# A shared selector for both halves of the state-space mask, and expert 0's rows from one-hot products

## The chip, the core and the metric

The kernel runs on one core of one Trainium2 chip. A core has five engines, each with an instruction queue of its own: TensorE (PE, matmuls and transposes; PEld is its loading of the stationary operand), VectorE (DVE), ScalarE (ACT), GpSimd (POOL) and SyncE (SP, which here only issues DMAs). They wait for each other through semaphores. The metric is the device time of one execution in microseconds; lower is better.

## The reference

The program is two transformer blocks on 512 tokens of width 1024. Only what the change touches is shown, shortened:

```python
# block 1, state-space part (SSD): 12 heads in 4 groups of 3, 4 chunks of 128 tokens
a_cs = cumsum(da)                                          # per chunk and head
seg  = a_cs[..., :, None] - a_cs[..., None, :]
lmat = exp(where(causal, seg, -inf))                       # 128 x 128 per chunk and head
y_diag = einsum('bclgn,bcsgn->bcgls', cm, bm) * lmat ...   # "mask" times C.B, then times x

# block 2, mixture of experts: 16 experts, 2 per token
h = h + concat(o_a, o_b) @ w_out
t = rms_norm(h, ffn_norm)
gates = route(t @ w_group + b_group, t @ w_expert + b_expert)
for e in range(16):
    y += gates[:, e:e+1] * ((silu(t @ w_gate[e]) * (t @ w_up[e])) @ w_down[e])
return rms_norm(h + y, final_norm)
```

## The kernel before

Large products work on weights in units of 512 KB (128 x 1024 fp32). SP loads a unit into a ring of `raw` buffers; ACT copies it to a reduced-precision half `whi` and DVE (or POOL) subtracts to get the rest, `wlo` (`split`, L264). Each product is then three matmuls, hi x hi, hi x lo, lo x hi (`mm3`, L274, lines 276 to 278). The loads run ahead of the splits, and the splits ahead of PE, as far as the rings have room (`fill`). The recorded instructions are put in order by a scheduler that knows costs and priorities; `issue_after` makes an instruction stand behind another, and `ahead(n)` raises its priority.

**The mask units** (`ssd_dt`, `ssd_mask_unit`, L776 to L848). `ssd_dt` transposes the 48 running sums (4 chunks x 12 heads) of a token chunk into rows, splits them into hi and lo parts, and spreads each over three columns of heads: `ssd_cH` and `ssd_cL`, 48 x 384 each. A selector `ssd_sel` (48 x 16, ones in the three rows that belong to a unit) picks a unit's rows. For each of 16 units PE sums into one bank: the causal mask (L840), selector x hi (L841), selector x lo (L842), and beside it C.B (L843). ACT then takes the exponent and DVE multiplies.

**From w_out_2 to expert 0** (L2005 to L2175). w_out_2 is computed in two halves of 512 columns (`projR`, L378). As each of four token tiles of the second half is added to `x` on DVE (L403), `after(tt)` transposes it, computes routing logits (`logits`: 4 fp32 matmuls of 20 columns against `rt_w`, L2028), the norm factor (`rstd`, with a power on POOL, L291) and the tile's choice of experts (`route_tile`). `ranks(tt)` counts the place of each token among its expert's tokens and makes the one-hot matrix `rt_oh` of expert 0: token by slot, 96 slots (L2049, bf16). Each tile of x times the norm gain is written to a DRAM table `xnd`.

After the fourth tile, `slots_row(0)` multiplies the one-hot with token numbers (L1833) to get the 96 row numbers `sn_i`, POOL gathers these rows from `xnd` into `ex_g` by an indirect DMA, PE transposes them (8 transposes, L1887), and ACT and DVE split them into `ex_xh` and `ex_xl`, on which expert 0's gate products run. The same is done for expert 1 (`sn_oh`, L2098). A small DMA `mark` writes expert 0's row numbers to DRAM (L2116) so that the weight loads behind it on SP wait until the numbers exist. Two weight splits have their `wlo` on POOL in this stretch (`s.plan`, L2088). `final_norm` is loaded as one row (`grow`) and spread over partitions by two fp32 matmuls against ones (L125). Later experts' rows are gathered two experts ahead, from the indices `sn_ix` that `route` computes.

Of the kernel before, what the change touches and what calls it, by code (L numbers as in the profile page):

```python
# [70 lines left out]
class Kern:  # L71
# [202 lines left out]
    def mm3(s, ps, a, asl, b, bsl, first, last):  # L274
        mm = s.nc.tensor.matmul
        mm(ps, a.hi[asl], b.hi[bsl], start=first, stop=False)  # L276
        mm(ps, a.hi[asl], b.lo[bsl], start=False, stop=False)  # L277
        mm(ps, a.lo[asl], b.hi[bsl], start=False, stop=last)  # L278
# [99 lines left out]
    def projR(s, src, ld, nk, get, x, after, tail=3, mid=None, lag=2, order=None):  # L378
# [4 lines left out]
        for half in range(2):  # L383
            cs = slice(half * 512, half * 512 + 512)
# [16 lines left out]
            for tt in range(NT):  # L401
                mms(ws, tt)
                nc.vector.tensor_add(x[:, tt, cs], x[:, tt, cs], pss[tt])  # L403
# [372 lines left out]
    def ssd_dt(s, pd, x):  # L776
# [32 lines left out]
        it = s.tmp.tile([48, 16], F32, name="ssd_it", tag="h")  # L809
        nc.gpsimd.iota(it, pattern=[[-3, 16]], base=0, channel_multiplier=1, allow_small_or_imprecise_dtypes=True)  # L810
        eq = s.tmp.tile([48, 4, 16], F32, name="ssd_eq", tag="h")
# [15 lines left out]
        for o, v in ((s.ssd_cs.hi, hi), (s.ssd_cs.lo, lo)):
            V.tensor_mul(o, v.bitcast(F32)[:, None, :].to_broadcast(sh), hm[:, :, None].to_broadcast(sh))
        yield

    def ssd_mask_unit(s, pl, c, g):
# [7 lines left out]
        sel = s.ssd_sel[:, u:u + 1].to_broadcast([48, P])  # L839
# [895 lines left out]
    def route(s, pool, tmp, g, ev):  # L1735
# [58 lines left out]
        for i in range(2):  # L1794
# [3 lines left out]
        V.tensor_tensor(oh, s.slot[:, None, :].to_broadcast([P, 8, CAP]),  # L1798
                        rk.rearrange("p i t -> p (i t)")[:, :, None].to_broadcast([P, 8, CAP]), OP.is_equal)
# [28 lines left out]
    def slots_row(s, pool, e, oh):  # L1828
# [7 lines left out]
        if e:  # L1836
            nc.scalar.activation(v, ps[:CAP, 0:2], AF.Copy)
        else:
            nc.vector.tensor_copy(v, ps[:CAP, 0:2])
        eng = nc.gpsimd if e else nc.vector  # L1840
        s.row_op = eng.tensor_scalar(ix, v[:, 0:1], v[:, 1:2], float(T), op0=OP.add, op1=OP.add).ins
# [138 lines left out]
    def moe(s, mixT):  # L1980
# [35 lines left out]
        oh = pr.tile([P, NT, CAP], BF16, name="rt_oh")  # L2016
# [76 lines left out]
        ix = []
        for e in range(XG):
            if e:
                oh = pn.tile([P, NT, CAP], BF16, name="sn_oh")
                sh = [P, NT, CAP]
                V.tensor_tensor(oh, s.slot[:, None, :].to_broadcast(sh), s.rk[:, :, e:e + 1].to_broadcast(sh), OP.is_equal)  # L2098
# [3 lines left out]
            if not e:  # L2102
                s.fence = [s.row_op]
        grow = s.tmp.tile([1, D], F32, name="grow", tag="h", bufs=1)
        with s.tc.issue_after(hi_op):
            nc.scalar.dma_start(grow, dap(A["final_norm_2"], 0, [[D, 1], [1, D]]))
        with s.tc.issue_after(s.logit_op), s.tc.issue_after(hi_op):
            gf = s.bcast_pe(s.gain, grow, "gain")
# [6 lines left out]
        mark = s.dram.tile([CAP, 1], I32, name="mark")  # L2115
# [212 lines left out]
```

## Time and profile before

| | |
|---|---|
| Median of 3 runs | 1455.51 us (1454.84 to 1457.64) |
| Profiled execution | 1453.98 us, its span 1452.2 us |
| PE busy | 1399.7 us, 96% of the span |
| DVE, ACT, POOL busy | 977.7, 779.2, 103.8 us |
| Chain that ended last, by engine | PE 86%, DVE 6%, ACT 3%, DMA 2% |
| Mean granted clock of PE | 0.987 |

A span is the time from the first to the last instruction of one execution that the profiler recorded. A busy share is an average over the whole program; what a stretch is bound by is read from that stretch. The chain starts at the last instruction and follows back what each step waited for. "issue to landing" of a DMA is the time from its issue until its completion is seen. The granted clock is PE's clock as a share of full speed; its two levels are 1.2 and 2.4 GHz.

### The profile page before, as it was taken

The numbers are of one execution on the slowest core, as the hardware profiler recorded it, in microseconds if no ns is written. First come the engines' busy times: TensorE is split into PE (matmuls) and PEld (weight loads), VectorE is DVE, ScalarE is ACT, GpSimd is POOL, SyncE is SP. The second block draws the span as 40 slices with busy tenths as digits, with TensorE's granted clock in tenths as the row PEclk, the third lists the DMA queues.
The fourth block names the chain that finished last, engine by engine and source line by source line (L and its number), as shares of the span: only waits on it lengthen the run. The fifth ranks groups of instructions, "written<-read, shape, count | busy, mean of one in ns | idle before, by whom it ended". The sixth has DMA issues, their size and how long they took to land.

```text
span 1452.2 us, 20178 instructions
## 1 busy us (share of the span) xinstructions
PE 1399.7 (96%) x7467; PEld 1130.2 (78%) x7467; DVE 977.7 (67%) x1772; ACT 779.2 (54%) x1200; POOL 103.8 (7%) x103
## 2 busy tenths in 40 slices
PE   7999999999999999999999999999998599999996
PEld 6888887787879888888888889877887367777774
DVE  6989577565465444444365997766555599999997
ACT  6465654434334333233344685554443388888885
POOL 1000000010010000000000400000102111111111
PEclk9999999999999999999999999999999699999998
DMA  7353342521223333323232423120754899999993
GB/s 199 92 136 112 90 131 73 174 88 58 75 71 116 102 95 94 101 88 100 89 101 87 134 74 88 41 77 18 260 204 172 226 357 356 353 343 349 349 349 130
DMA packets 145933, 223.51 MB, mean 154 GB/s; under 512 B 18466, under 2 KB 71106, under 8 KB 145816
## 3 DMA queue, kind: packets, MB, share of 16 engines
q1 hardware_dynamic: 136852, 200.48, 42.7%
q0 software_dynamic: 3568, 10.34, 3.0%
q10 hardware_dynamic: 5412, 11.37, 2.2%
q8 instruction: 59, 0.97, 0.3%
q14 instruction: 42, 0.34, 0.1%
HBM read 208.41 MB, written 14.95 MB: 154 GB/s over the span
## 4 chain that ended last, share of the span: by engine, by line
PE 86%; DVE 6%; ACT 3%; DMA 2%; issue 2%; POOL 1%; DVEq 0%; SPq 0%; ACTq 0%; POOLq 0%
PE mm L276 24%; PE mm L278 24%; PE mm L277 24%; PE sm L1416 2%; PE tr L1548 1%; PE tr L323 1%; PE tr L1887 1%; PE sm L1532 1%; POOL rs_r L291 1%; DMA ex_g<-xnd,sn_i 1%; DVE wlo L271 1%; PE sm L879 1%; PE sm L276 1%; PE tr L1540 1%; PE sm L2028 1%
## 5 line engine op out<-in xcount | busy, mean ns | idle before, releaser
L271 DVE TENSOR_TENSOR wlo<-raw,whi 128x1024 fp32r<-128x1024 f32 (+1 forms) x351 | 423.6, 1222 | 216.4 <-ACT whi L270 213.5
L270 ACT ACTIVATE whi<-raw 128x1024 fp32r<-128x1024 f32 (+1 forms) x356 | 372.7, 1057 | 293.2 <-PE mm L277 154.0
L276 PE MATMUL mm<-hT_hi,whi 128*128 128x512 f32 (+1 forms) x768 | 283.2, 369 | 1.9 <-DVE x L403 1.7
L278 PE MATMUL mm<-hT_hi,wlo 128*128 128x512 f32 (+1 forms) x768 | 281.5, 367 | 0.0
L277 PE MATMUL mm<-hT_lo,whi 128*128 128x512 f32 (+1 forms) x768 | 280.9, 366 | 0.0
L276 PE MATMUL mm<-whi,hT_hi 128*128 128x512 f32 (+1 forms) x592 | 219.7, 371 | 1.4 <-ACT hT_hi L315 1.4
L278 PE MATMUL mm<-whi,hT_lo 128*128 128x512 f32 (+1 forms) x592 | 217.9, 368 | 0.0
L277 PE MATMUL mm<-wlo,hT_hi 128*128 128x512 f32 (+1 forms) x592 | 217.0, 367 | 0.0
L278 PEld LDWEIGHTS mm<-hT_hi,wlo 128*128 128x128 f32 x768 | 144.7, 188 | 24.3
L276 PEld LDWEIGHTS mm<-hT_hi,whi 128*128 128x128 f32 x768 | 144.3, 188 | 24.8 <-DVE x L403 1.9
L277 PEld LDWEIGHTS mm<-hT_lo,whi 128*128 128x128 f32 x768 | 144.6, 188 | 23.3
L276 PEld LDWEIGHTS mm<-whi,hT_hi 128*128 128x128 f32 x592 | 111.8, 189 | 20.7 <-ACT hT_hi L315 2.3
L278 PEld LDWEIGHTS mm<-whi,hT_lo 128*128 128x128 f32 x592 | 111.7, 189 | 19.2 <-issue 0.6
L277 PEld LDWEIGHTS mm<-wlo,hT_hi 128*128 128x128 f32 x592 | 112.0, 189 | 18.5 <-issue 1.0
L276 PE MATMUL mm<-whi,ex_xh 128*96 128x512 f32 x256 | 102.8, 402 | 1.3 <-ACT ex_xh L315 0.6
L291 POOL TENSOR_TENSOR rs_r<-rs_v,mhalf 128x1 f32<-128x1 f32 (+2 forms) x42 | 33.4, 798 | 980.2 <-DVE rs_v L289 823.9
L277 PE MATMUL mm<-wlo,ex_xh 128*96 128x512 f32 x256 | 101.4, 396 | 0.0
L278 PE MATMUL mm<-whi,ex_xl 128*96 128x512 f32 x256 | 100.9, 395 | 0.0
L276 PEld LDWEIGHTS mm<-whi,ex_xh 128*96 128x96 f32 x256 | 41.5, 162 | 19.0 <-ACT ex_xh L315 1.1
L278 PEld LDWEIGHTS mm<-whi,ex_xl 128*96 128x96 f32 x256 | 41.6, 162 | 18.1
L277 PEld LDWEIGHTS mm<-wlo,ex_xh 128*96 128x96 f32 x256 | 41.8, 163 | 16.9
L1246 DVE SCALAR_TENSOR_TENSOR cv<-mm,cols,cv 128x511 f32<-128x511 f32 (+1 forms) x44 | 33.0, 749 | 30.0 <-ACT cv L1243 29.2
(568 smaller groups left out, 2060.3 us busy)
## 6 DMA issues: line engine op xcount, KB each, us to landing
raw<-in_w_gate SPq DMA_DIRECT2D x64, 512.0 KB
raw<-in_w_up SPq DMA_DIRECT2D x64, 512.0 KB
raw<-in_w_down SPq DMA_DIRECT2D x64, 512.0 KB
raw<-in_ffn_w_up SPq DMA_DIRECT2D x44, 512.0 KB
raw<-in_w_in SPq DMA_DIRECT2D x40, 512.0 KB
raw<-in_ffn_w_down SPq DMA_DIRECT2D x22, 512.0 KB
raw<-in_w_out SPq DMA_DIRECT2D x16, 512.0 KB
raw<-in_w_in SPq DMA_DIRECT2D x8, 520.0 KB
```

The costliest lines, as they stand in the source:

```text
L270: s.hi_op = s.nc.scalar.activation(hv, v, AF.Copy).ins
L271: eng.tensor_sub(lv, v, hv.bitcast(F32))
L276: mm(ps, a.hi[asl], b.hi[bsl], start=first, stop=False)
L277: mm(ps, a.hi[asl], b.lo[bsl], start=False, stop=False)
L278: mm(ps, a.lo[asl], b.hi[bsl], start=False, stop=last)
L291: s.pow_op = nc.gpsimd.tensor_tensor(r, v, s.mhalf[:, :n], OP.pow).ins
L323: nc.tensor.transpose(ps[:, i * P:(i + 1) * P], src[:, (k0 + i) * P:(k0 + i + 1) * P], s.ident)
L879: nc.tensor.matmul(yd[:, o:o + 64], L[:, j], xdt[:, h], start=True, stop=True)
L1246: V.scalar_tensor_tensor(y[:, d:], ps[:, :512 - d], cw[:, w:w + 1], y[:, d:], op0=OP.mult, op1=OP.add)
L1416: nc.tensor.matmul(ps[:, sl], qk[:, sl], qk[:, sl], start=True, stop=True)
L1532: nc.tensor.matmul(ps[:, :n], qa[:, h, sl], ka[:, h, :n], start=True, stop=False)
L1540: nc.tensor.transpose(pt[:, j * P:j * P + P], p[:, j * P:j * P + P], s.ident)
```

## The change

The state-space part keeps hi and lo rows in one tile: the 48 sums are copied twice into a zeroed 128 x 128 tile (columns 0 to 47 and 64 to 111), transposed at once, and the upper 64 rows take the hi part, the lower 64 the lo part. The selector has 128 rows with the same ones in both halves, so one matmul of 128 rows takes the place of the two of 48.

Expert 0's rows are no longer gathered. The one-hot matrix of expert 0 is kept in fp32 and multiplied with x itself: `first(tt)` has 8 fp32 matmuls per tile (stationary: 128 columns of x, moving: the tile's 96 one-hot columns) that accumulate over the four tiles into two banks `p0` the transposed rows of expert 0. ACT and DVE take them out in 8 pieces each, with the norm gain as a scale, into `ex_xh` and `ex_xl`. Expert 1 is gathered as before; its one-hot is made tile by tile beside that of expert 0, and its row numbers are made on DVE. `mark`, the first gather, its transposes and the wide one-hot are gone; the two `wlo` that POOL made are made on DVE, behind the additions of tiles 0 and 1; `final_norm` is spread by one DMA on POOL's queue behind the last power. The one-hot of the 8 remaining parts of `route` now stands behind expert 1's row numbers, and expert 1's transposes behind a product of expert 0.

```diff
-        pt = s.ptr.tile([P, 512], F32, name="tr")
-        nc.tensor.transpose(pt[:48, 0:P], cs[:, 0].rearrange("p a b -> p (a b)"), s.ident)
...
+        c2 = s.tmp.tile([P, P], F32, name="ssd_c2", tag="h")
+        V.memset(c2, 0.0)
+        for r in (0, 64):
+            V.tensor_copy(c2[:, r:r + 48], cs[:, 0].rearrange("p a b -> p (a b)"))
         pt = s.ptr.tile([P, 512], F32, name="tr")
+        nc.tensor.transpose(pt[:, 0:P], c2, s.ident)
...
-        nc.tensor.matmul(o, sel, s.ssd_cs.hi.rearrange("p j t -> p (j t)"), start=False, stop=False)
-        nc.tensor.matmul(o, sel, s.ssd_cs.lo.rearrange("p j t -> p (j t)"), start=False, stop=True)
+        nc.tensor.matmul(o, s.ssd_sel[:, u:u + 1].to_broadcast([P, P]), s.ssd_cs.rearrange("p j t -> p (j t)"),
+                         start=False, stop=True)
...
+        def first(tt):
+
+            for b in range(2):
+                for k in range(4):
+                    c = (4 * b + k) * P
+                    nc.tensor.matmul(p0[b][:, k * CAP:(k + 1) * CAP], x[:, tt, c:c + P], oh[0][:, tt],
+                                     start=tt == 0 and k == 0, stop=tt == 3 and k == 3)
...
-            V.tensor_scalar(oh[:, tt], s.slot, s.rk[:, tt, 0:1], None, op0=OP.is_equal)
+            for e in range(2):
+                V.tensor_scalar(oh[e][:, tt], s.slot, s.rk[:, tt, e:e + 1], None, op0=OP.is_equal)
...
+            if tt == 3:
+                p0.extend(s.pmm.tile([P, 512], F32, name="mm") for _ in range(2))
+                for i in range(3):
+                    first(i)
...
+        gf = s.gain.tile([P, D], F32, name="gain")
+        with s.tc.issue_after(s.pow_op):
+            nc.gpsimd.dma_start(gf, dap(A["final_norm_2"], 0, [[0, P], [1, D]]))
         ranks(3)
+        first(3)
...
-        s.plan = [(nc.gpsimd, []), (nc.gpsimd, [s.pow_op])]
+        s.plan = [(V, [s.add_ops[0]]), (V, [s.add_ops[1]])]
+        late, s.late = s.late, 1000
         s.fill(most=L3, splits=2)
...
-            with s.tc.issue_after(s.rank_op):
-                ix.append(s.slots_row(pn, e, oh))
-            s.gather(xgs[e], ix[e])
...
+        with s.tc.issue_after(s.rank_op):
+            ix1 = s.slots_row(pn, 1, oh[1])
+        s.gather(xgs[1], ix1)
...
-        mark = s.dram.tile([CAP, 1], I32, name="mark")
-        with s.tc.issue_after(nc.sync.dma_start(mark, ix[0]).ins):
-            s.fill()
+        s.fence = [s.row_op]
+        s.fill()
         s.late = FL[5]
-        xT = s.expert_pick(pe, xgs[0])
+        xT = s.expert_xT(pe)
+        for k in range(KD):
+            ps = p0[k // 4][:, k % 4 * CAP:k % 4 * CAP + CAP]
+            gk = s.cols2[:, 96 + k:97 + k]
+            nc.scalar.activation(xT.hi[:, k], ps, AF.Copy, scale=gk)
+            V.scalar_tensor_tensor(xT.lo[:, k], ps, gk, xT.hi[:, k].bitcast(F32), op0=OP.mult, op1=OP.subtract)
...
-            xT = s.expert_pick(pe, xgs[(e + 1) % XG])
+            with s.tc.issue_after(s.gate_op) if e == 0 else nullcontext():
+                xT = s.expert_pick(pe, xgs[(e + 1) % XG])
```

The order of the instructions moves with this. The first place is a mask unit on PE; `neg_lt` is the causal mask, `BT` and `CT` are the B and C of the chunk. Before:

```order
755 L864 MATMUL tr<-ident,BT 128x128 x4
756 L840 LDWEIGHTS identb
757 L840 MATMUL sm<-neg_lt,identb 128x384
758 L841 MATMUL sm<-ssd_cH,ssd_sel 128x384
759 L842 MATMUL sm<-ssd_cL,ssd_sel 128x384
760 L843 MATMUL sm<-CT,BT 128x128
761 L276 MATMUL mm<-memT_hi,whi 128x256
```

And after the change:

```order
754 L872 MATMUL tr<-ident,BT 128x128 x4
755 L848 LDWEIGHTS identb
756 L848 MATMUL sm<-neg_lt,identb 128x384
757 L849 MATMUL sm<-ssd_cH,ssd_sel 128x384
758 L851 MATMUL sm<-CT,BT 128x128
759 L276 MATMUL mm<-memT_hi,whi 128x256
```

The unit has one matmul less, and nothing stands in its place.

The second place is PE from the last product of w_out_2 to expert 0's first gate products. `tr<-ident,x` are the transposes of tile 3, `rt_h` its transposed half for the logits, `rt_u` and `rt_o` belong to the ranks, `rt_tb` holds token numbers. Before:

```order
4916 L278 MATMUL mm<-whi,hT_lo 128x512
4917 L2023 MATMUL tr<-ident,x 128x128 x4
4918 L2028 MATMUL sm<-rt_w,rt_h 128x20 x4
...
4932 L1732 MATMUL sm<-rt_Mb,rt_u 128x16
...
4934 L1833 MATMUL sm<-rt_tb,rt_oh 96x2
...
4942 L1833 MATMUL sm<-rt_tb,sn_oh 96x2
...
4957 L125 MATMUL mm<-grow,ones 128x512 x2
4958 L1887 MATMUL tr<-ident,ex_g_9992 128x96 x8
4959 L276 MATMUL mm<-whi,ex_xh 96x512
4960 L277 MATMUL mm<-wlo,ex_xh 96x512
```

And after the change, where `rt_oh_9468` is the fp32 one-hot of expert 0 and `rt_oh_9469` the bf16 one of expert 1:

```order
4900 L278 MATMUL mm<-whi,hT_lo 128x512
4901 L2034 MATMUL mm<-rt_oh_9468,x 128x96 x15
4902 L2042 MATMUL tr<-ident,x 128x128 x4
4903 L2034 MATMUL mm<-rt_oh_9468,x 128x96
4904 L2047 MATMUL sm<-rt_w,rt_h 128x20 x4
...
4911 L2034 MATMUL mm<-rt_oh_9468,x 128x96 x8
...
4919 L1740 MATMUL sm<-rt_Mb,rt_u 128x16
...
4934 L2034 MATMUL mm<-rt_oh_9468,x 128x96 x8
...
4936 L1842 MATMUL sm<-rt_tb,rt_oh_9469 96x2
4937 L276 MATMUL mm<-whi,ex_xh 96x512
4938 L277 MATMUL mm<-wlo,ex_xh 96x512
4939 L278 MATMUL mm<-whi,ex_xl 96x512
```

Fifteen of the sixteen products of tiles 0 and 1 stand ahead of tile 3's transposes, tile 2's behind its ranks, tile 3's directly ahead of the gate; the matmuls on `grow` and the transposes of `ex_g` are gone.

The third place is DVE between the tables of tile 2 (`h`) and the addition of tile 3 (L403 before, L404 after). Before:

```order
1195 L2073 TENSOR_TENSOR h<-x,gain 128x1024
1196 L301 SCALAR_TENSOR_TENSOR rs_t<-rs_r,rs_h 128x1
1197 L306 SCALAR_TENSOR_TENSOR rt_r<-rs_t,rs_r 128x1
1198 L1733 TENSOR_TENSOR rt_rk<-sm,rt_Mb 128x16
1199 L2061 SCALAR_TENSOR_TENSOR rt_la<-sm,rt_r,rt_b 128x20
1200 L2049 TENSOR_SCALAR rt_oh<-rt_s,rt_rk 128x96
1201 L2063 SCALAR_TENSOR_TENSOR rt_lgg<-sm,rt_r,rt_la 128x4
1202 L2064 SCALAR_TENSOR_TENSOR rt_lge<-sm,rt_r,rt_la 128x16
1203 L1715 TENSOR_REDUCE rt_gm<-rt_lgg 128x1
1204 L403 TENSOR_TENSOR x<-x,mm 128x512
```

And after the change:

```order
1194 L2097 TENSOR_TENSOR h<-x,gain 128x1024
1195 L271 TENSOR_TENSOR wlo<-raw,whi 128x1024 x2
1196 L298 TENSOR_SCALAR rs_h<-rs_v 128x1
1197 L1741 TENSOR_TENSOR rt_rk<-sm,rt_Mb 128x16
1198 L301 SCALAR_TENSOR_TENSOR rs_t<-rs_r,rs_h 128x1
1199 L2069 TENSOR_SCALAR rt_oh_9468<-rt_s,rt_rk 128x96
1200 L306 SCALAR_TENSOR_TENSOR rt_r<-rs_t,rs_r 128x1
1201 L2069 TENSOR_SCALAR rt_oh_9469<-rt_s,rt_rk 128x96
1202 L2085 SCALAR_TENSOR_TENSOR rt_la<-sm,rt_r,rt_b 128x20
1203 L404 TENSOR_TENSOR x<-x,mm 128x512
```

The two `wlo` that POOL made stand here on DVE, ahead of tile 1's ranks and the addition of tile 3; the one-hot comparison stands there twice.

## Rows read from the trace of the kernel before

**Rows 1.** The page, busy shares by engine and the costliest group of instructions
```profile
PE 1399.7 (96%) x7467; PEld 1130.2 (78%) x7467; DVE 977.7 (67%) x1772; ACT 779.2 (54%) x1200; POOL 103.8 (7%) x103
...
L271 DVE TENSOR_TENSOR wlo<-raw,whi 128x1024 fp32r<-128x1024 f32 (+1 forms) x351 | 423.6, 1222 | 216.4 <-ACT whi L270 213.5
```

**Rows 2.** Windows: stretch, length; busy of each engine; PEclk, DMA share, GB/s
```profile
173.00:257.00 84.00, 83.59 (x538) 70.39 (x538) 63.97 (x101) 46.99 (x98) 1.66 (x3) 1.00 0.32 101
1110.00:1160.00 50.00, 31.57 (x156) 22.29 (x155) 30.02 (x108) 17.88 (x27) 13.00 (x9) 0.73 0.81 234
1130.00:1146.00 16.00, 4.97 (x18) 2.33 (x17) 5.21 (x24) 2.51 (x5) 3.42 (x3) 0.50 0.92 160
1200.00:1300.00 100.00, 100.00 (x480) 71.11 (x479) 92.45 (x92) 85.92 (x103) 14.16 (x12) 1.00 1.04 353
```

**Rows 3.** The chain of waits, 1115 to 1165 us: start, length, what
```profile
1130.83 14.23 DMA ex_g<-xnd,sn_i
...
1148.65 0.43 PE mm L278
```

**Rows 4.** PE's timeline, end of w_out_2 to expert 1: start, length, what
```profile
1117.33 0.96 PE L2028 MATMUL sm<-rt_w,rt_h 128*128 128x20 f32 x8
...
1121.43 0.66 PE L2023 MATMUL tr<-ident,x 128*128 128x128 f32 x4 [2.54 <-DVE x L403]
1122.77 1.90 PE L2028 MATMUL sm<-rt_w,rt_h 128*128 128x20 f32 x8 [0.69 <-ACT rt_h L2025]
...
1146.62 0.74 PE L276 MATMUL mm<-whi,ex_xh 128*96 128x512 f32 x1
...
1159.72 0.83 PE L1887 MATMUL tr<-ident,ex_g 96*128 96x96 f32 x8
```

**Rows 5.** DVE's timeline, the same stretch
```profile
1118.61 1.83 DVE L2049 TENSOR_SCALAR rt_oh<-rt_s,rt_rk 128x96 bf16<-128x96 f32 x1
...
1124.87 1.32 DVE L301 SCALAR_TENSOR_TENSOR rs_t<-rs_r,rs_h 128x1 f32<-128x1 f32 x1
...
1128.92 0.26 DVE L2049 TENSOR_SCALAR rt_oh<-rt_s,rt_rk 128x96 bf16<-128x96 f32 x1
```

**Rows 6.** POOL's timeline, the same stretch
```profile
1118.03 2.35 POOL L271 TENSOR_TENSOR wlo<-raw,whi 128x1024 fp32r<-128x1024 f32 x1 [1.13 <-ACT whi L270]
```

**Rows 7.** PE's timeline in the first mask unit
```profile
174.28 0.34 PE L842 MATMUL sm<-ssd_cL,ssd_sel 48*128 48x384 f32 x1
174.55 0.49 PE L843 MATMUL sm<-CT,BT 128*128 128x128 f32 x2
```

**Rows 8.** PE's timeline at fp32 products of 128 columns
```profile
1024.19 1.08 PE L1446 MATMUL sm<-hg_v,hg_PT 128*128 128x128 f32 x8
1025.10 1.06 PE L1453 MATMUL sm<-hg_v,hg_kd 128*128 128x128 f32 x8
```

**Rows 9.** DMA from 1076 to 1165: busy tenths, GB/s; issues, us to landing
```profile
DMA  9993604300046605545399980964899999578999
GB/s 400 369 391 120 233 0 108 135 0 0 0 156 266 285 0 236 236 186 225 103 399 404 277 307 7 68 42 41 301 302 269 303 386 388 148 251 254 285 303 321
...
ex_g<-xnd,sn_i POOLq DMA_INDIRECT x2, 14.4
ex_g<-xnd,sn_ix POOLq DMA_INDIRECT x2, 8.4
```

**Rows 10.** SP's timeline, two places of the weight stream
```profile
1152.42 0.37 SPq L212 DMA_DIRECT2D raw<-in_w_gate  x1
...
1398.31 11.90 SPq L212 DMA_DIRECT2D raw<-in_w_down  x8
```

**Rows 11.** L1887, gathered rows transposed: ns min/median/max, first and last start
```profile
L1887 PE MATMUL tr<-ident,ex_g x128: 243/246/420, 1145.1 to 1404.2; 96*128 96x96 f32 x128
```

**Rows 12.** ACT's timeline, the last weight splits
```profile
1427.98 2.00 ACT L270 ACTIVATE whi<-raw 128x1024 fp32r<-128x1024 f32 x2
```

**Rows 13.** SP's waits, 1100 to 1452 us: total, times, longest us
```profile
SPq L212 <- DVE rt_y L1805: 11.6, 1, 11.6
```

More of the change, by code (lines that the diff above doesn't have):

```diff
@@ L277, in mm3 @@
         mm(ps, a.hi[asl], b.lo[bsl], start=False, stop=False)
-        mm(ps, a.lo[asl], b.hi[bsl], start=False, stop=last)
+        return mm(ps, a.lo[asl], b.hi[bsl], start=False, stop=last).ins
     def rstd(s, ss, n, width, pool, v0=None, out=None):
@@ L383, in projR @@
         for half in range(2):
+            adds = s.add_ops = []
             cs = slice(half * 512, half * 512 + 512)
@@ L402, in projR @@
                 mms(ws, tt)
-                nc.vector.tensor_add(x[:, tt, cs], x[:, tt, cs], pss[tt])
+                adds.append(nc.vector.tensor_add(x[:, tt, cs], x[:, tt, cs], pss[tt]).ins)
                 if half:
@@ L807, in ssd_dt @@
         yield
-        it = s.tmp.tile([48, 16], F32, name="ssd_it", tag="h")
-        nc.gpsimd.iota(it, pattern=[[-3, 16]], base=0, channel_multiplier=1, allow_small_or_imprecise_dtypes=True)
-        eq = s.tmp.tile([48, 4, 16], F32, name="ssd_eq", tag="h")
+        it = s.tmp.tile([P, 16], F32, name="ssd_it", tag="h")
+        for r in (0, 64):
+            nc.gpsimd.iota(it[r:r + 64], pattern=[[-3, 16]], base=0, channel_multiplier=1,
+                           allow_small_or_imprecise_dtypes=True)
+        eq = s.tmp.tile([P, 4, 16], F32, name="ssd_eq", tag="h")
         for j in range(3):
@@ L1797, in route @@
             V.tensor_reduce(rk[:, i], x, AX.X, OP.add)
[L1798 to L1799 removed]
+        with s.tc.issue_after(s.row_op):
+            V.tensor_tensor(oh, s.slot[:, None, :].to_broadcast([P, 8, CAP]),
+                            rk.rearrange("p i t -> p (i t)")[:, :, None].to_broadcast([P, 8, CAP]), OP.is_equal)
         pt = s.psm.tile([P, 512], F32, name="sm")
@@ L1835, in slots_row @@
         ix = pool.tile([CAP, 1], I32, name=f"sn_i{e}")
[L1836 to L1841, printed above, removed]
+        nc.vector.tensor_copy(v, ps[:CAP, 0:2])
+        s.row_op = nc.vector.tensor_scalar(ix, v[:, 0:1], v[:, 1:2], float(T), op0=OP.add, op1=OP.add).ins
         return ix
@@ L1896, in expert_gate, with expert_xT @@
             for k in range(2):
-                s.mm3(ps[:CAP], xT, (slice(None), k0 + k), w, (slice(None), k), k0 + k == 0, k0 + k == 7)
-        return ps
+                op = s.mm3(ps[:CAP], xT, (slice(None), k0 + k), w, (slice(None), k), k0 + k == 0, k0 + k == 7)
+            if k0 == 4:
+                s.gate_op = op
+        return ps
+    def expert_xT(s, pool):
+        return Split(pool.tile([P, KD, CAP], F32R, name="ex_xh", bufs=1),
+                     pool.tile([P, KD, CAP], F32R, name="ex_xl", bufs=1))
     def expert_pick(s, pool, xg):
-        xT = Split(pool.tile([P, KD, CAP], F32R, name="ex_xh", bufs=1),
-                   pool.tile([P, KD, CAP], F32R, name="ex_xl", bufs=1))
+        xT = s.expert_xT(pool)
         s.pick(xg, lambda k0, ps: s.put_split(ps, xT.hi[:, k0:k0 + 4], xT.lo[:, k0:k0 + 4]))
@@ L2015, in moe @@
         s.rr = pr.tile([P, NT], F32, name="rt_r")
-        oh = pr.tile([P, NT, CAP], BF16, name="rt_oh")
+        oh = [pr.tile([P, NT, CAP], (F32, BF16)[e], name=f"rt_oh{e}") for e in range(2)]
+        p0 = []
+        def first(tt):
[4 more added lines that the diff above has]
+                                     start=tt == 0 and k == 0, stop=tt == 3 and k == 3)
         def logits(tt, half):
@@ L2086, in moe @@
         s.release()
-        hi_op = None
-        s.plan = [(nc.gpsimd, []), (nc.gpsimd, [s.pow_op])]
+        s.plan = [(V, [s.add_ops[0]]), (V, [s.add_ops[1]])]
+        late, s.late = s.late, 1000
         s.fill(most=L3, splits=2)
-        hi_op = s.hi_op
+        s.late = late
         with s.tc.issue_after(s.last_h):
             s.fill(most=1, splits=0)
[L2093 to L2098, printed above, removed]
-            with s.tc.issue_after(s.rank_op):
-                ix.append(s.slots_row(pn, e, oh))
-            s.gather(xgs[e], ix[e])
[L2102 to L2108, printed above, removed]
+        with s.tc.issue_after(s.rank_op):
+            ix1 = s.slots_row(pn, 1, oh[1])
+        s.gather(xgs[1], ix1)
         for tt in range(AL, NT):
```

21 lines of the change are left out of this document (11 added, 10 removed).

## The prediction

> **What bounds the kernel now.** I read the page's busy shares first: TensorE (PE) is busy 96% of the span [rows 1], so a saving must either be PE work taken away where PE has no gap, or a stretch where PE waits. The windows show one of each [rows 2]. In 173 to 257 us, where the 16 mask units lie, PE is busy 83.59 of 84.00 us while VectorE (DVE) has 20 us free: PE is the limit there. In 1130 to 1146 us PE is busy 4.97 of 16 us and its granted clock is 0.50, the lower level of 1.2 GHz; from 1200 us on it is busy without a gap. The chain of waits names the hole [rows 3]: 14.23 us from the issue of expert 0's gather at 1130.83 to its landing, then the transposes of the gathered rows. PE's timeline gives the frame [rows 4]: w_out_2's products end at 1118.9 (the transposes of tile 3 begin at 1121.43 after 2.54 us idle), expert 0's first gate product starts at 1146.62. So 27.7 us pass between the last large product and the next one. Two of the small steps in it are stretched: on DVE the one-hot comparison took 1.83 us and a one-column step 1.32, where the same comparison took 0.26 at 1128.92 [rows 5]; both stand beside a weight split on POOL of 2.35 us, one of two (the other at 1123.82) [rows 6]. That these slow each other is my reading of the coincidence, not shown.
>
> **Part 1, the mask selector.** Each of the 16 units loses its L842 matmul; the L841 one now has 128 rows instead of 48. From the start of L842 to the start of L843 is 0.27 us [rows 7]; this is the first of 16 alike, all of them in the window where PE is the limit: 16 x 0.27 = 4.3 us. That the taller matmul takes longer is not shown here: 384-column matmuls start 0.27 us apart with 48 rows [rows 7], and I take that for 128 rows too. Added on DVE are a memset, two 48-column copies and taller forms of the selector's small steps. The nearest rows, 0.26 us for 96 columns [rows 5], give some 0.8 us; DVE has the 20 us free, but the setting up happens before the window, so I count 0.4. Sum: **-3.9 us**, between -5 (the taller form costs nothing, the freed weight loads help) and -1.5 (DVE ends last for part of the units).
>
> **Part 2, expert 0's rows.** Removed from the path: index row, gather, 8 transposes, that is 1129.2 to 1146.6. Added to PE: 32 fp32 products of 96 columns. An fp32 matmul stands in the trace as two instructions; 4 of them with 128 columns start at 1024.19 and the next line starts at 1025.10 [rows 8], so 0.23 us each, and 4 of 20 columns took 0.96 us in all [rows 4], 0.24 less the tail. I take 0.22, ends 0.20 and 0.23, at the full clock.
>
> Now the path, step by step. The order puts 15 products (tiles 0 and 1, all but one) ahead of tile 3's transposes: 1118.9 + 15 x 0.22 = 1122.2. The addition they must wait for today ends at 1121.4; in the new order DVE carries both weight splits itself (2 x 1.22 us by the mean of the page's first group [rows 1], with no POOL beside it), but saves the stretch of 1.83 - 0.26. So the transposes start at 1122.2, 0.8 late. Copying to SBUF goes as now; the logits take 0.96 instead of 1.90 if the clock holds [rows 4], so they end 0.1 early, at 1124.5. The route of tile 3 follows on DVE: today from 1124.67 to its one-hot at 1129.2 (4.5 us), now without the stretch of 1.32 - 0.22, with one more comparison of 0.26 for each of two tiles: 1128.4. Tile 2's 8 products lie inside that route (1.8 us on an idle PE); tile 3's 8 end 1.8 us behind it, and the copies of the first bank start when it closes, half way. Expert 0's first product then starts near **1129.5 to 1130, against 1146.62: -17.0**.
>
> What is given back or gained behind it:
> - The first products of expert 0 run 0.43 us apart today [rows 3], at the lower clock; some 7 of them at half of that return 7 x 0.2 = 1.4 us.
> - DVE gets crowded. It works 30.0 of the 50 us from 1110 to 1160 [rows 2]. Two splits (2.4), four fp32 one-hots (1.0) and 8 pieces of ex_xl (8 x 0.26) come to it, 1.6 goes (the wide one-hot, two put_splits): 34 us of work for about 33 us until expert 1. Not all of it must be done by then, since splits run ahead of PE. I take 1.0 us lost, ends 0 and 5.
> - Expert 1's gather is issued near 1130.5, as now. The two early gathers took 14.4 us to land and the later ones 8.4 [rows 9]: 1138.9 to 1144.9; expert 0's gate and up products end near 1141.5. By the nearer row (nothing else but loads runs beside it) it costs nothing; by the other 3.4.
> - `mark` and SP's wait for it go. Right behind it, in four slices of 2.2 us, DMA moved 7, 68, 42 and 41 GB/s, in one of them at a busy share of 0.9 or more, between slices of 300 and more [rows 9]: the loads and the gather crept for 7 us beside 96 four-byte writes. The Trainium skill (DMA: Bandwidth & Descriptors, Specifications) says that transfers under 512 B are read, modified and written; by it the stall belongs to `mark` and the gather lands in 8.4. The rows show only that both lie together.
> - The broadcast load of final_norm (512 KB, on POOL's queue) replaces two matmuls that lay in the gather's shadow: cost nothing, hidden by the loads' lead below; without that lead, the time of one load, 1.65 us by the rows below.
>
> Sum: -17.0 - 1.4 + 1.0 = -17.4, with part 1 **-21.3 us**. The profiled execution took 1453.98 us (span 1452.2), so 1432.7; the median of the runs shown lies 1.5 above that execution, so **1434 us**.
>
> **What is late next: the weights.** SP issues a load at 1152.42 and, 149 loads later, one at 1398.31 [rows 10]: 1.65 us each. PE takes a unit in 1.46 us: 16 sets of 8 transposes, the last done at 1404.2 [rows 11], the second set at 1159.72 [rows 4], so 14 experts of 12 units lie between. So the lead shrinks by 0.19 us per unit, 30 us over the phase, and the last load is issued by 1410.2 where the last two units are split from 1427.98 [rows 12]. If the loads stayed where they are while PE came 21 us earlier, PE would want the last at 1407 before it is issued; with the 8.4 us of a transfer that is 11 us lost. They should not stay: SP stood 11.6 us for one buffer that a route step held [rows 13] and that step comes earlier, `mark` no longer holds the queue, and part 1 moves everything. I take the stream as moved by the same 17 us. The windows show 353 GB/s through this phase [rows 2]. The Trainium skill (same page and section) gives some 358 GB/s as what HBM serves one core; by it a stream that starts late never catches up.
>
> **Rivals.**
> - *DVE becomes the bound of the first two experts.* For it: 34 us of work in 33, and 92.45 of 100 us busy behind it, so a delay heals slowly [rows 2]. Against: only xl and the first splits are wanted at once. 5 us lost instead of 1.0: 1438.
> - *The clock falls anyway.* For it: it stands at 0.50 today in the hole [rows 2], where PE had worked in short pieces with waits between; the new products are such pieces too. Against: 15 of them stand without a gap just where PE idles today. Tile 3's and 2's products at twice the time (3.6), the logits (1.0) and the first products (1.4) come back, and half of tile 0 and 1's (1.6): +7.5, 1441. The Trainium skill (TensorE: Matmul & The Clock Gate, HAM oscillation) warns of just this, bursts with waits between them that fall back each time; the half clock from the logits on (0.96 to 1.90) agrees with it.
> - *The weights do not move.* +11 at most: 1445. The same place gives the slower side: if loads went at 1.83 us instead of 1.65 (149 x 0.18 = 27 us: the 17 by which the stream moves, and the 10 that lie today between the last landing, 1409.6 + 8.4, and its split), PE would end later than today. For it: the queues are full (share 1.04). Against: the change adds 0.5 MB and removes 0.4.
> - *Expert 1's gather is the new wait*, 14.4 us again: +3.4, 1437.5.
> - *Part 1 does nothing*, DVE being last in the mask stage: +3.9, 1438.
>
> **How the numbers follow.** Forecast 1434 (own range 1430 to 1438) 0.58; DVE 0.12; clock 0.10; weights late 0.06, of which 0.02 within a hair of today; gather 0.06; part 1 idle 0.04; slower 0.04. The range from 1428 (1.1 more from part 1, DVE's 1.0, the products at 0.20, and some 3 us by which the steps of the path may come shorter) to 1443 (the clock case and 2 us of another) leaves out the weights and the slower case. A measurement of this kernel tells about 0.2% (2.9 us) from no change: faster 0.94, same 0.02, slower 0.04.
>
> **What would show it.** PE's window from 1118 to 1130 (less 4 for part 1) at clock 1.00 and mostly busy; no DMA wait ahead of expert 0's gate, and its first product near 1126; first products 0.2 apart; 15 products of 0.22 us; no L842 twin, and the mask stage 4 us shorter; gathers at 8.4; SP without the 11.6 us wait. The forecast is wrong if PE waits for DVE (xl, wlo) or ACT in the first two experts, if the last experts wait for a load, or if the lower clock covers the products.

## The result: 1434.6 us against 1455.3

The changed kernel took 1434.63 us in the median of 4 runs (1432.39 to 1436.88), the kernel before 1455.32 (4 runs, 1454.84 to 1457.64): a ratio of 0.9855, 95% interval 0.9836 to 0.9873. Forecast were 1434 us and a range of 1428 to 1443. The total is right. Of its terms one was less than half of what it should have been, one was too large, and a fall of the clock that the forecast had nowhere near the mask units took part of the first away again.

The profiled execution of the changed kernel is the longest of its four: 1436.88 us, span 1435.1, beside 1453.98 and 1452.2 of before, so 17.1 us. The page, busy shares and the chain that ended last, stands against [rows 1]:

```profile
PE 1399.3 (98%) x7499; PEld 1140.7 (79%) x7499; DVE 977.3 (68%) x1786; ACT 777.1 (54%) x1202; POOL 98.9 (7%) x101
...
PE 88%; DVE 6%; ACT 2%; issue 1%; POOL 1%; DMA 0%; SPq 0%; DVEq 0%; POOLq 0%; ACTq 0%
```

PE's busy time is the same (1399.7 before) in a span that is 17 us shorter. That is a sum of opposite changes: the mask matmuls went, the one-hot products and two stretches at the lower clock came, and the rest of what went is idle time. The chain has no DMA left. PE's timeline from the end of w_out_2 to experts 0 and 1 (start, length, what), against [rows 4]:

```profile
1115.60 3.48 PE L2034 MATMUL mm<-rt_oh,x 128*128 128x96 f32 x30
1118.92 0.60 PE L2042 MATMUL tr<-ident,x 128*128 128x128 f32 x4
...
1120.20 1.07 PE L2047 MATMUL sm<-rt_w,rt_h 128*128 128x20 f32 x8 [0.49 <-ACT rt_h L2044]
...
1121.94 2.91 PE L2034 MATMUL mm<-rt_oh,x 128*128 128x96 f32 x16 [0.60 <-DVE rt_oh L2069]
...
1125.53 3.73 PE L2034 MATMUL mm<-rt_oh,x 128*128 128x96 f32 x16
1129.06 0.21 PE L1842 MATMUL sm<-rt_tb,rt_oh 128*96 128x2 bf16 x1
1129.13 0.71 PE L276 MATMUL mm<-whi,ex_xh 128*96 128x512 f32 x1
...
1132.61 0.48 PE L276 MATMUL mm<-whi,ex_xh 128*96 128x512 f32 x1 [0.68 <-ACT ex_xh L2137]
...
1144.31 0.48 PE L276 MATMUL mm<-whi,ex_xh 128*96 128x512 f32 x1 [1.46 <-ACT ex_xh L315]
```

Two records are one product, since each stands as two instructions. The first 15 products start 3.32 us ahead of tile 3's transposes, 0.22 each, as forecast. From the end of w_out_2 to expert 0's gate it is 1129.13 - 1115.60 = 13.5 us, where it was 27.7. (Here and below this is counted from the start of the first product; from the end that the trace gives w_out_2's last matmul, where the 27.7 begins, it is 0.2 us less.) Tile 3's eight products need 3.6 us, not 1.8: their clock is the lower level. The windows (stretch, length; busy of each engine; granted clock, DMA share, GB/s), against [rows 2]:

```profile
150.00:155.00 5.00, 5.00 (x36) 4.65 (x35) 3.03 (x11) 1.15 (x3) 1.01 (x2) 0.51 0.00 0
155.00:160.60 5.60, 5.60 (x42) 5.15 (x41) 1.21 (x1) 0.86 (x2) 0.00 (x0) 0.50 0.00 0
...
1119.00:1122.00 3.00, 1.91 (x19) 1.65 (x17) 1.56 (x12) 2.43 (x3) 1.13 (x2) 1.00 0.85 274
1122.00:1123.00 1.00, 1.00 (x9) 1.00 (x10) 1.00 (x9) 0.40 (x1) 0.00 (x0) 0.94 1.02 408
1123.00:1129.00 6.00, 5.90 (x36) 5.73 (x36) 2.61 (x19) 0.56 (x2) 0.00 (x0) 0.50 1.04 410
```

PE was busy 1.91 of 3 us, then its clock went to 0.50 (1.2 GHz) although it now worked without gaps, and came back by 1130. A second stretch at 0.50, from 150.0 to 163.6, lies ahead of the mask units, in the S5 part, the other state-space layer of block 1. PE's longest waits from 1100 us on (total, times, longest):

```profile
PE mm L276 <- ACT ex_xh L315: 1.5, 1, 1.5
PE mm L276 <- ACT ex_xh L2137: 0.7, 1, 0.7
PE mm L2034 <- DVE rt_oh L2069: 0.6, 1, 0.6
```

The load of `final_norm` and the gathers, 1076 to 1165 us (count, us from issue to landing), against [rows 9]:

```profile
gain<-in_final_norm POOLq DMA_DIRECT2D x1, 512.0 KB, 7.5
ex_g<-xnd,sn_ix POOLq DMA_INDIRECT x3, 8.0
ex_g<-xnd,sn_i POOLq DMA_INDIRECT x1, 8.7
```

SP's wait that stands against [rows 13]:

```profile
SPq L212 <- PE sm L1842: 8.2, 1, 8.2
```

None of PE's three longest waits is for a DMA, gathers land in 8 to 9 us instead of 14.4, and the 11.6 us for which SP stood behind `rt_y`, a tile of the route, are replaced by 8.2 behind the row numbers of expert 1.

**Where the time went.** The start of the same weight split on ACT (L270), counted from the first as 0, in before, and how much earlier (-) or later it starts in other kernels. The last five columns are experiments told below; e5_after is the changed kernel once more.

| split | before at | after | e1 | e5 | e7 | e9 | e11 |
|---|---|---|---|---|---|---|---|
| 24, S5 ends | 157.2 | +6.8 | +2.1 | +2.1 | +0.7 | +6.7 | +0.8 |
| 60, masks done | 395.3 | -3.0 | -7.0 | -6.6 | -8.6 | -3.0 | -8.1 |
| 132 | 812.5 | -3.1 | -6.2 | -5.8 | -7.7 | -2.2 | -7.2 |
| 204, experts | 1203.3 | -17.6 | -8.2 | -20.6 | -23.0 | -18.6 | -24.4 |
| 348, near the end | 1415.6 | -17.2 | -8.2 | -20.2 | -22.6 | -18.2 | -24.0 |

Between splits 24 and 60, where the mask units lie, every kernel with part 1 gains 8.8 to 9.9 us; forecast were 3.9. Between 132 and 204 part 2 gains 14.5 in the profile of after; forecast were 17.4. Ahead of split 24 the stretch at 0.50 costs 6 us in the executions that have it.

### The profile page after: what moved, and what is told of

Same layout as the page of the kernel before. It is cut to its first block, busy times and chain, and to the rows that moved or that the text cites. A ratio compares the mean times of both kernels' runs of the same rounds, so it can differ in the third digit from the quotient of the medians.

```text
span 1435.1 us, 20243 instructions
## 1 busy us (share of the span) xinstructions
PE 1399.3 (98%) x7499; PEld 1140.7 (79%) x7499; DVE 977.3 (68%) x1786; ACT 777.1 (54%) x1202; POOL 98.9 (7%) x101
## 4 chain that ended last, share of the span: by engine, by line
PE 88%; DVE 6%; ACT 2%; issue 1%; POOL 1%; DMA 0%; SPq 0%; DVEq 0%; POOLq 0%; ACTq 0%
PE mm L276 25%; PE mm L278 24%; PE mm L277 24%; PE sm L1424 2%; PE tr L323 1%; POOL rs_r L291 1%; PE tr L1556 1%; PE tr L1892 1%; PE sm L1540 1%; PE sm L887 1%; DVE cv L1032 1%; PE mm L2034 1%; DVE wlo L271 1%; PE sm L276 1%; PE sm L750 1%
## 5 line engine op out<-in xcount | busy, mean ns | idle before, releaser
L270 ACT ACTIVATE whi<-raw 128x1024 fp32r<-128x1024 f32 (+1 forms) x356 | 373.0, 1057 | 290.4 <-PE mm L277 152.4
L278 PEld LDWEIGHTS mm<-hT_hi,wlo 128*128 128x128 f32 x768 | 144.8, 188 | 24.4
```

The costliest lines, as they stand in the source:

```text
L270: s.hi_op = s.nc.scalar.activation(hv, v, AF.Copy).ins
L278: return mm(ps, a.lo[asl], b.hi[bsl], start=False, stop=last).ins
```

## The experiments

**Each part alone.** e1_selector is the kernel before with part 1, e2_rows the changed kernel with the old selector. My theory was that the parts add up, with the sizes of the forecast.

> The kernel before with the mask selector alone (part 1), expert 0's rows still gathered. Additive theory: the 16 removed matmuls are worth 16 x 0.27 = 4.3 us less what the setting up costs, so 3 to 4 us faster than before, and the last weight split ahead of w_out_2 stands 3.0 to 3.9 us earlier. Rival, that the mask stage was really held by VectorE: 0 to 1 us faster, with new PE waits for L847's tiles. The gather wait in front of expert 0 stays at some 11 us in PE's waits by either.

> The changed kernel with the old selector of 48 rows and two matmuls per mask unit (part 2 alone). Additive theory: the rest of the gain, 16 to 18 us faster than before, that is 3 to 4 us slower than the changed kernel. Rival, that the two parts interact through the order of the first 260 us: clearly less or more than that, and then the sum of the two single gains differs from 20.7 us by over 3 us.

e1 took 1446.03 us, 0.9933 (0.9914 to 0.9952) of before: 10.5 us off, where 3 to 4 were expected. e2 took 1442.39, 0.9907 (0.9891 to 0.9924): 14.1, where 16 to 18 were. The one is some 9 us by the table. The rest of e1 lies in the hole, in its wait for the gather, which was expected to stay at 11 us (before: 11.0; why it is shorter in e1 isn't shown):

```profile
PE tr L1893 <- DMA ex_g<-xnd,sn_i: 8.1, 1, 8.1
```

10.5 and 14.1 make 24.6, and the whole change 20.7 by the first runs and 22.3 by e5_after's (1456.3 to 1434.0). The rival asked for a sum more than 3 us away from 20.7, and 24.6 is 3.9 away; but the intervals of e1 and e2 are 2.8 and 2.4 us to either side, so the times don't decide it. The profiles show one overlap of the right size: the gather's 2.9 us count in e1 and again in e2, which has no such gather.

**What a mask unit costs.** Why 9 and not 3.9? In before the rest of the unit around [rows 7] (PE's timeline):

```profile
173.75 0.33 PE L840 MATMUL sm<-neg_lt,identb 128*128 128x384 bf16 x1
174.01 0.44 PE L841 MATMUL sm<-ssd_cH,ssd_sel 48*128 48x384 f32 x1
...
174.79 0.36 PE L276 MATMUL mm<-memT_hi,whi 128*128 128x256 f32 x1
```

From the first start to the next line's it takes 1.04 us. In after the same unit:

```profile
180.19 0.33 PE L848 MATMUL sm<-neg_lt,identb 128*128 128x384 bf16 x1
180.22 0.47 PE L849 MATMUL sm<-ssd_cH,ssd_sel 128*128 128x384 f32 x1
180.53 0.39 PE L851 MATMUL sm<-CT,BT 128*128 128x128 f32 x2
180.67 0.36 PE L276 MATMUL mm<-memT_hi,whi 128*128 128x256 f32 x1
```

0.48 us: 0.56 less, by 16 units 9.0; the other 15 units of either kernel agree with these to 0.01. More went than one matmul of 0.27. The weight loads of before say what (PEld's timeline, in brackets the idle time in front):

```profile
174.00 0.18 PEld L841 LDWEIGHTS sm<-ssd_cH,ssd_sel 48*128 48x128 f32 x1 [0.26 <-issue]
174.11 0.18 PEld L842 LDWEIGHTS sm<-ssd_cL,ssd_sel 48*128 48x128 f32 x1
174.55 0.30 PEld L843 LDWEIGHTS sm<-CT,BT 128*128 128x128 f32 x2 [0.25 <-issue]
```

And PEld's waits in before, 169 to 257 us, in sum:

```profile
PEld sm L843 <- issue: 4.0, 16, 0.3
PEld sm L841 <- issue: 3.6, 16, 0.3
```

At each change of the stationary's rows, 128 to 48 and back, PEld stands 0.23 and 0.25 us in the mean (3.6 and 4.0 by 16) with nothing in the trace to wait for; between the two loads of 48 rows it does not. Theory: the change of row count costs this, and part 1 takes both away. Rival: it is the second matmul as such. e8_pad keeps two matmuls of 128 rows each, the unused half zero:

```diff
-        s.ssd_cs = pd.tile([P, 3, P], F32R, name="ssd_cH")
+        s.ssd_cs = [pd.tile([P, 3, P], F32R, name="ssd_c" + i) for i in ("H", "L")]
...
+            V.tensor_scalar_mul(s.ssd_cs[i][z], hl[z, i].bitcast(F32)[:, None, :].to_broadcast(sh), 0.0)
...
+        for i in range(2):
+            nc.tensor.matmul(o, s.ssd_sel[:, u:u + 1].to_broadcast([P, P]), s.ssd_cs[i].rearrange("p j t -> p (j t)"),
+                             start=False, stop=i == 1)
```

> The changed kernel with two matmuls per mask unit again, hi and lo apart, but both with 128 rows (the other half of the rows zero): the number of matmuls of before, the row count of after. Theory that most of part 1's gain is the change between 48 and 128 rows and not the matmul: a unit costs 0.16 to 0.20 us more than in the changed kernel, not 0.56, so the kernel is 2.5 to 3.5 us slower than the changed one, and the weight loads of the unit show no idle for issue. Rival, that the count of matmuls is what costs: all of part 1's gain goes, 8 to 10 us slower than the changed kernel.

It took 1437.65 us, 0.9865 (0.9843 to 0.9887), 3.7 above the changed kernel beside it; the intervals touch, so the unit on PE's timeline decides:

```profile
174.88 0.33 PE L850 MATMUL sm<-neg_lt,identb 128*128 128x384 bf16 x1
174.91 0.47 PE L852 MATMUL sm<-ssd_cH,ssd_sel 128*128 128x384 f32 x1
175.22 0.34 PE L852 MATMUL sm<-ssd_cL,ssd_sel 128*128 128x384 f32 x1
175.39 0.38 PE L854 MATMUL sm<-CT,BT 128*128 128x128 f32 x2
175.53 0.36 PE L276 MATMUL mm<-memT_hi,whi 128*128 128x256 f32 x1
```

0.65 us (14 of the other 15 units agree to 0.01, one is followed by other work), and no idle of that kind left on PEld. So of the 0.56 us that a unit lost, 0.17 is the matmul and 0.39 the two changes of row count. The table's stretch agrees: between splits 24 and 60 e8 gains 5.7 us on before, the kernels with one matmul 8.8 to 9.9. The Trainium skill (TensorEngine Tiling (Array Packing), Key Properties) says that changing the tiling mode drains TensorE; it gives no price, and the trace agrees if 48 rows are loaded in another mode than 128.

**`mark` and the gather.** The forecast suspected `mark` behind the slow gather of before. e3_nomark is the kernel before without it:

```diff
-        mark = s.dram.tile([CAP, 1], I32, name="mark")
-        with s.tc.issue_after(nc.sync.dma_start(mark, ix[0]).ins):
-            s.fill()
+        s.fill()
```

> The kernel before without the small DMA that writes expert 0's row numbers to DRAM; the weight loads behind it no longer stand behind that write, the gathers stay. Theory that the 96 four-byte writes clog the DMA engines: the two early gathers land in 8 to 9 us instead of 14.4, PE's wait ahead of expert 0 falls from 11 to 5 us, the kernel is 5 to 6 us faster, a third of part 2's gain. Rival, that the gather is slow because of the loads and the table writes that run beside it: it still takes 13 us or more, and the time is within 1.5 us of before.

It took 1451.51 us, 0.9968 (0.9954 to 0.9981), 5.0 off, with this wait of PE for the gather:

```profile
PE tr L1887 <- DMA ex_g<-xnd,sn_i: 4.6, 1, 4.6
```

And what DMA moved from 1076 to 1165 us (GB/s in 40 slices, as in [rows 9]), with the gathers of experts 0 and 1, in us to landing:

```profile
GB/s 387 334 354 271 92 151 0 227 16 0 0 0 236 322 149 114 223 134 239 238 161 325 398 265 372 356 399 362 311 291 377 47 13 244 255 298 334 327 319 267
...
ex_g<-xnd,sn_i POOLq DMA_INDIRECT x2, 9.2
```

With `mark` the gather took 14.4 us, without it 9.2. The edit takes away two things, the 96 writes of four bytes and the place of the weight loads behind them (issued from 1130.49 in before, from 1124.89 in e3), and no run has the one without the other. That the writes are what slows the gather rests on the rate: in the four slices where before moved 7, 68, 42 and 41 GB/s [rows 9], for most of them with loads and gathers issued, e3 moved 372, 356, 399 and 362. Of the change's 14 us in the hole, 5 were to be had by deleting three lines.

**The splits on POOL.** e4_pool puts the two `wlo` back on POOL:

```diff
-        s.plan = [(V, [s.add_ops[0]]), (V, [s.add_ops[1]])]
+        s.plan = [(nc.gpsimd, []), (nc.gpsimd, [s.pow_op])]
```

> The changed kernel with the two weight splits of this stretch back on POOL. Theory that a split on POOL stretches VectorE's small steps beside it: single steps of 1 to 2 us appear again among those of 0.2, POOL's two splits take some 2.35 us each, and the step from the end of w_out_2 to expert 0 gets 1 to 2 us longer, so the time is 1 to 2 us above the changed kernel. Rival, that the stretch was chance or that PE's products cover it: within 0.7 us of the changed kernel or faster, because 2.4 us of work leave VectorE.

It took 1437.73 us, 0.9871 (0.9852 to 0.9889), 3 more than the change, with intervals that overlap. The trace shows the mechanism. POOL's timeline in e4_pool:

```profile
1117.43 2.35 POOL L271 TENSOR_TENSOR wlo<-raw,whi 128x1024 fp32r<-128x1024 f32 x1
```

DVE's, at the same time:

```profile
1117.51 2.29 DVE L301 SCALAR_TENSOR_TENSOR rs_t<-rs_r,rs_h 128x1 f32<-128x1 f32 x1 [0.49 <-POOL rs_r L291]
```

And PE's behind it:

```profile
1120.72 0.22 PE L1739 MATMUL sm<-rt_Mb,rt_o 128*128 128x16 bf16 x3 [1.98 <-DVE rt_lge L2088]
...
1122.78 3.73 PE L2034 MATMUL mm<-rt_oh,x 128*128 128x96 f32 x16
```

A step of one column stands on DVE until POOL's split is over (1119.80 and 1119.78); the same step is 0.22 us in after. PE then idles 1.98 us, and the products behind run at 0.50, as they do in the profile of after. From w_out_2 to the gate e4 needs 16.1 us (1110.23 to 1126.37), the changed kernel 13.5. What the forecast called a coincidence in [rows 5] and [rows 6] is a cause: there, too, both stretched steps end within 0.1 us of POOL's split (1120.44 and 1120.38, 1126.19 and 1126.17). The Trainium skill (SBUF — State Buffer, SBUF: two separate sides) has it as an exclusive lock on a port pair: the loser stands for the whole instruction. The trace agrees, 2.29 beside 2.35.

**What sets the start of expert 0's gate.** In after the products, at 0.50, end when the gate starts. e5_after is the same kernel in another execution, where the clock held:

> The changed kernel as it is, to stand beside the next three on the same chip. Expected 1434 to 1437 us; its profiled execution shows by its granted clock whether the lower level in the first 180 us (13.6 us long in the first profile of this kernel) belongs to the kernel or to that execution: if to the kernel, it is there again at about 150 us.

1433.97 us, 0.985 (0.9827 to 0.9874). PE's timeline:

```profile
1121.91 2.02 PE L2034 MATMUL mm<-rt_oh,x 128*128 128x96 f32 x16
...
1125.65 0.48 PE L276 MATMUL mm<-whi,ex_xh 128*96 128x512 f32 x1 [1.71 <-ACT ex_xh L2137]
```

And ACT's:

```profile
1125.26 0.34 ACT L2137 ACTIVATE ex_xh<-mm,cols 128x96 fp32r<-128x96 f32 x1 [4.20 <-DMA xnd<-hl]
```

The products take 0.12 per record again, and PE waits 1.71 us all the same. `ex_xh` lies in memory that `hl`, tile 3's rows for the table, held before; ACT may write it only when the DMA to `xnd` has read it, 9.7 us after its issue at 1115.58, beside the stream of weights. `rt_y` on DVE stands 3.1 us for the same transfer. In after this wait was there too, hidden by the slow products. No row of before shows it, since the gather took longer than any of this.

e6_order tries to win time ahead of tile 3's transposes, by products of tiles 1 and 2 behind the logits:

```diff
-                for i in range(3):
-                    first(i)
+                first(0)
+                with s.tc.issue_after(o):
+                    first(1)
+                with s.tc.issue_after(o):
+                    first(2)
```

> The changed kernel with the one-hot products of tiles 1 and 2 ordered behind tile 3's logits instead of ahead of its transposes. Theory that products ahead of the transposes delay the path and that the waits behind them let the clock fall: transposes of tile 3 start 1.3 to 1.6 us earlier after w_out_2, the products fill the two waits of 0.5 and 0.6 us, and expert 0's first product comes 1.5 us earlier, 3 us if the clock stays up: 1.5 to 3 us faster than the changed kernel. Rival, that VectorE's ranks set the end of this stretch and not PE: within 0.7 us of the changed kernel.

1433.53 us, 0.984 (0.9819 to 0.9861): nothing that can be told from e5. In its profile the logits do start 1.5 us sooner behind w_out_2 than in after, but the gate 12.8 us behind it (1116.52 to 1129.28), as in e5: some of the products that now stand behind the logits ran at the lower clock (0.57 from 1122 to 1126 us), and PE still waits 0.46 us for `ex_xh`, which starts 9.7 us after the transfer's issue. e7_pick moves the other wait, 1.46 us at 1144.31, where ACT did a table load (1.28 us) and expert 0's `ex_h` ahead of expert 1's rows:

```diff
...
-            h = s.expert_h(pe, pg, pu, sl[e][0][:, 1:2])
+            with s.tc.issue_after(xT.last[0]) if e == 0 else nullcontext():
+                h = s.expert_h(pe, pg, pu, sl[e][0][:, 1:2])
```

> The changed kernel with ScalarE taking out expert 1's rows ahead of expert 0's activation, with its table load of 1.28 us. Theory that PE's 1.5 us wait ahead of expert 1 is that table load and the activation behind it: the wait falls below 0.7 us, and the kernel is 0.8 to 1.5 us faster. Rival, that the gather sets that place: the wait stays and turns into one for the DMA, the time the same within 0.5 us.

1431.72 us, 0.9839 (0.9816 to 0.9862); the wait fell to 0.86, not below 0.7. The median is 2 us lower than e5's, not beyond the intervals.

Then the transfer itself. e9_table issues it on ACT's queue, with the write of `acc` behind it, and the load of `final_norm` an expert later:

```diff
-                s.last_h = nc.sync.dma_start(s.xnd[tt * P:(tt + 1) * P, :], hs[tt]).ins
+                s.last_h = nc.scalar.dma_start(s.xnd[tt * P:(tt + 1) * P, :], hs[tt]).ins
...
-        with s.tc.issue_after(s.pow_op):
-            nc.gpsimd.dma_start(gf, dap(A["final_norm_2"], 0, [[0, P], [1, D]]))
...
+            with s.tc.issue_after(s.last_h):
+                nc.scalar.dma_start(s.acc[tt * P:(tt + 1) * P, :], x[:, tt])
...
+            if e == 1:
+                with s.tc.issue_after(s.g_ins):
+                    nc.gpsimd.dma_start(gf, dap(A["final_norm_2"], 0, [[0, P], [1, D]]))
```

> The changed kernel, with two transfers moved: the last table write (xnd from hl, which held the memory that expert 0's ex_xh reuses) is issued from ACT's queue instead of behind the weight loads on SP, with the write of acc behind it, and the load of final_norm is issued in the loop of expert 1 instead of in the hole. Theory (at full clock the start of expert 0's gate is set by that table write, 1.7 to 1.9 us of wait in two profiles): the write lands sooner than the 9.8 us it took, the wait ahead of expert 0's gate falls to under 0.5 us when the clock holds, and the time is 1 to 2 us under the changed kernel (1432 to 1433). Rival (the write only shares its bandwidth with the weight loads and takes as long from any queue): no change of the wait, 1434.

> e9_table and e7_pick together, without the other order of the products. If the two waits add up (1.7 to 1.9 us at the table write, 0.6 to 1.5 at expert 1's rows): 2.5 to 3.5 us under the changed kernel, 1430.5 to 1431.5. If they hide each other, no better than e7_pick alone (1431.7).

> e9_table, with the products of tiles 1 and 2 behind tile 3's logits (as in e6_order) and expert 1's rows taken out ahead of expert 0's ex_h on ACT (as in e7_pick). If the table write is what hid the gain of e6_order, the three together give 3 to 4 us under the changed kernel: 1430 to 1431. If the order costs PE more at half clock than it saves in front of the transposes: no better than e11_table_pick.

e9 took 1432.42 us, 0.984 (0.9824 to 0.9857); e11, e9 and e7 together, 1431.69, 0.9836 (0.9818 to 0.9854). PE's timeline in e9's profile:

```profile
1116.57 3.48 PE L2034 MATMUL mm<-rt_oh,x 128*128 128x96 f32 x30
...
1125.60 2.02 PE L2034 MATMUL mm<-rt_oh,x 128*128 128x96 f32 x16
...
1127.61 0.47 PE L276 MATMUL mm<-whi,ex_xh 128*96 128x512 f32 x1
```

And ACT's:

```profile
1127.22 0.34 ACT L2136 ACTIVATE ex_xh<-mm,cols 128x96 fp32r<-128x96 f32 x1 [2.48 <-DMA xnd<-hl]
```

The transfer takes 8.0 us (1119.27 to 1127.22) and still sets when `ex_xh` starts, but its first piece is ready when the products end, and PE waits for nothing: 11.0 us from w_out_2 to the gate, 27.7 in before. That is a gain of 16.7 where 17.0 was forecast. Which of the moves shortened the transfer wasn't told apart. e10_all, with the order of e6 as well, took 1435.89 (0.9839, 0.982 to 0.9859) in runs from 1430.15 to 1436.11: no better than e11. Its clock held here, so that isn't the expectation's reason: its `ex_xh` starts 8.1 us after the transfer's issue (1119.81 to 1127.87), PE waits 0.48 for it, and the gate comes 11.2 us behind w_out_2. The transfer still sets the gate. The best median is e11's, 25 us under before. By the median it is no better than e7 (1431.72), as its rival says, and beside the change (e5, 0.985) the intervals overlap: its profile has no wait at the gate and 0.86 at expert 1, but that it beats the change the times don't show.

**The clock.** The runs of one kernel lie in groups by their mean granted clock: e9 at 1431.95 to 1432.42 (0.995) and 1436.02, 1436.93 (0.991), e10 at 1430.15 and 1430.85 against 1435.89 to 1436.11. In all four profiles with the whole stretch at 0.50 in S5 (after, e6, e9 and e10; e1's has a shorter one), it begins near 150 us, behind a wait of PE for `s_H`; in e7 the same wait, 1.47 us against 1.49 in after, is followed by a clock of 1.00. The hole is alike: behind the same two waits of 0.49 and 0.60 us the clock fell in the profiles of after and e8 and held in those of e5, e7, e9 and e11. So the waits alone don't decide, and I have no experiment that tells what does. It stays open whether the change makes the fall in S5 more frequent: the profiles of before, e2 and e3, without part 1, don't have it, nor do those of e4, e5, e7, e8 and e11, with it.

## Why the forecast was right, and where it wasn't

- **Part 1, -3.9: mis-sized; -9 was there.** The step that failed is "from the start of L842 to the start of L843 is 0.27 us" as the price of what goes. Its row was read by itself: the unit's other starts, also 0.26 to 0.27 apart, and the idle time of the weight loads show that 0.39 of each unit's 0.56 us was the change of row count. PE's busy share, 83.59 of 84.00 us [rows 2], hides this: L840's record of 0.33 us reaches over the start of L841, which comes 0.26 later in before and 0.03 later in after. The bound of -5 was too tight: "the freed weight loads help" was priced without looking at PEld's rows. Nor is 0.27 the price of a 384-column matmul of 128 rows: a second one among its like adds 0.17 (e8_pad, 175.22 to 175.39).
- **The clock in S5: not in the sum.** It took back 6 us in the profile of after. The forecast's rival on the clock had its place in the hole and not here; the two errors of the mask stage cancel in that execution and not in others.
- **The path, -17.0: the mechanism was right, the size fell short at one step.** 3.3 us for 15 products, 0.22 each, and no DMA wait were as forecast. "Tile 3's end 1.8 us behind" the route was 3.6 at the lower clock (after), and at the full clock the transfer from `hl` stood in the way (e5, 1.71). Either way 13.5 or 12.8 us instead of 10.7. The copies didn't start when the first bank closed, half way, as the path has it: in the profiles of after, e5, e6, e7, e9, e10 and e11 they start when the transfer has landed. With the shorter transfer, e9 has 11.0.
- **The rival "the clock falls anyway" came half true:** from 1122.9 on instead of the whole way, 2.6 us (2.91 and 3.73 for the products of tiles 2 and 3 where e5 has 2.02) instead of 7.5, and not in every execution. Its reason against, products without a gap at the head, held for the first 15.
- **Behind the gate, -0.4 in sum: nearly.** From expert 0's first product to expert 1's it took 15.2 us, before 14.6 (1146.62 to 1161.19): PE's wait for ACT ahead of expert 1, 1.46 us where before has 0.65, and one of 0.68 in expert 0 cost more than the clock returned. By e7 the table load with `ex_h` is 0.6 of the 1.46; in before it was over ahead of expert 1's transposes (1155.95 to 1157.23). It isn't DVE that is late there, as the rival had it, but ACT.
- **Weights and expert 1's gather: as forecast.** The stream moved with the rest (the last load is issued at 1394.8, in before at 1409.6), the gathers took 8.7 and 8.0, and no product waited for them. SP still stood, for 8.2 us instead of 11.6. That a late stream never catches up, as the forecast has it by 358 GB/s, these runs don't bear out: from 1123 to 1129 us DMA moved 410 GB/s in after.
- **The total** came out through opposite errors: 5 us too little in the masks, 2.6 to 2.9 too much in the hole (14.8 in e5 and 14.5 in after, of 17.4), and the fall in S5 in some of the runs.

## What to carry to other kernels

Price an edit by the starts of everything from the instruction ahead of it to the one behind it, and look at the weight loads' idle time too, since a busy share near 100% doesn't show it: where a matmul has another row count than its neighbours, joining it to them saves the changes as well. When a long wait is removed, ask which memory the first instruction behind it writes and who still reads that; such a wait doesn't show in the old profile. And before a wait on a transfer is designed away, look for small transfers beside it.

## What the runs showed of the hardware

- A change of the stationary operand's rows from 128 to 48 and back left PEld idle 0.23 and 0.25 us in the mean (before); net it cost 0.39 us per unit of two changes (e8_pad).
- Beside 96 writes of four bytes, with the weight loads behind them, a gather of 96 rows took 14.4 us, without them 9.2, and the run was 5.0 us shorter (e3_nomark).
- A DVE step of one column took 2.29 us beside a POOL subtraction of 2.35, and 0.22 without (e4_pool).
